# Attention's softmax reciprocals: a trip through DRAM in place of a ScalarE copy and transposes

## The chip, the cores and the metric

The kernel runs on one core of one Trainium2 chip. Time is device time in microseconds (us). A core has TensorE (PE, with its weight loads PEld), VectorE (DVE), ScalarE (ACT), GpSimd (POOL) and SyncE (SP). Here SP issues nearly all DMAs, in one queue that goes strictly in order: when an issue on SP has to wait, everything behind it waits too.

## What is computed

One layer over 2048 positions of width 1024, all in float32. The part that matters here is one of two groups of heads:

```
h   = RMSNorm(x);  z = h @ W_in
A   = gated MLP heads (8 heads)
B   = softmax(q k^T / 8 + c[t] - c[s]) v   for s <= t, 8 heads of width 64
x   = x + concat(A, B) @ W_out
x   = x + ConvFFN(RMSNorm(x));  out = RMSNorm(x)
```

Each row of the softmax has to be divided by its sum. The kernel multiplies the finished row of `p v` by the reciprocal of that sum.

## The kernel before

Every large product is made of three float32r matmuls (high and low parts). TensorE runs the projections, attention, the output projection, and the feed-forward layers one after the other. Attention is no phase of its own: a generator, `b_stream`, is advanced by one step after every 3.5 to 4.4 matmuls of the main work, so that attention's small matmuls lie between the main ones from about 120 us to 1470 us. `need` runs the generator on without waiting where the main work needs a finished block of 512 queries.

The pieces are (head `h`, query block `tb` of 512), eight heads in each of four blocks. A piece has two halves. `b_max` computes the scores with queries on partitions, and gets for each query the maximum and the sum of exponentials; its last instruction (L773, or L775 for `tb` = 0) writes the four reciprocals of each partition to the tile `rr`, which one pair of heads shares. `b_mix` computes the scores again with keys on partitions, and from them `p v` with the head's channels on partitions and queries along the free axis (tile `o` in PSUM). So the reciprocals lie on the wrong axis: query 128 a + p has its reciprocal on partition p, column a, and is wanted in column 128 a + p of all 64 partitions of its head. Pieces overlap: the order is `b_max` of a piece, then `b_mix` of the piece before it. `turn`, which `b_max` returns, is called at the fourth step of that `b_mix` and transposes the maxima (L779).

At the end of the second head of a pair, `b_mix` spreads the pair's reciprocals: ScalarE copies each of them 64 times into the tile `rw` (L835), the generator yields, four 128x128 transposes (L183, in `transpose4`) bring them into a PSUM bank, and VectorE multiplies the pair's `op` by that bank (L838). The result is split in two parts (tags `ph`, `pl`) and stored to `mixh` and `mixl`, from which the output projection loads it (`thi`, `tlo`). There are 16 pairs.

The bank comes from `scores`, which deals out three banks with the tag `s`, and later two more with the tag `dn`; attention's scores use the same ones. Keys come by `b_keys`: `m1` and `m2` (written `m<-kx` in the trace), and `v<-vd` for `b_mix`. There are two `m1` tiles, so the load of a key block has to wait on SP until TensorE is through with the block before the last. The order of instructions on each engine, SP's included, is fixed when the kernel is built, by a planner that works from a model of each instruction's and each transfer's time; a step's instructions go ahead of the main work's with a priority (`AHEAD_B`).

Of the kernel before, what the change touches and what calls it, by code (L numbers as in the profile page):

```python
# [8 lines left out]
F32 = mybir.dt.float32  # L9
F32R = mybir.dt.float32r  # L10
BF16 = mybir.dt.bfloat16
AF = mybir.ActivationFunctionType
ALU = mybir.AluOpType
# [5 lines left out]
P = 128  # L19
# [33 lines left out]
def f32(ap):  # L53
    return ap.bitcast(F32)
# [26 lines left out]
class Block:  # L81
# [134 lines left out]
    def constants(self):  # L216
        nc, a, tc = self.nc, self.a, self.tc
        cp = self.cpool = self.ctx.enter_context(tc.tile_pool(name="const", bufs=1))
        self.ident = cp.tile([P, P], F32, name="ident")
        make_identity(nc, self.ident)  # L220
        self.mhalf = cp.tile([P, 8], F32, name="mhalf")
        nc.gpsimd.memset(self.mhalf, -0.5)
        self.cols = cp.tile([P, 200], F32, name="cols")
        self.halo = cp.tile([P, 2 * NF, 2], F32, name="halo")
        nc.gpsimd.memset(self.halo, 0.0)
        dp = self.ctx.enter_context(tc.tile_pool(name="dram", bufs=1, space=DRAM))
        self.ones_d = dp.tile([2, HALF], F32, name="ones_d")
        t = lambda n, k, s: [dp.tile(s, F32, name=f"{n}{i}") for i in range(k)]
        self.qx = t("qx", 2, [8, 128, HALF])
        self.kx = t("kx", 2, [8, 132, HALF])  # L230
        self.cc = t("cc", 2, [8, 2, HALF])
        self.vd = t("vd", 2, [HALF, 8, P])
        self.mixh = t("mixh", 4, [D, TB])
        self.mixl = t("mixl", 4, [D, TB])
        self.rows_d = [t(f"rows{i}_", 8, [P, D]) for i in range(2)]
        self.act_d = [t(f"act{i}_", NF, [P, HALF]) for i in range(2)]
        self.tw_d = t("tw", NF // 2, [P, 2, D])

    def columns(self):

        nc, a = self.nc, self.a
        self.dma(self.cols, a["cols"])
        self.g_mix, self.g_ffn, self.sgb, self.cw0, self.cw1, self.cw2, self.cb = [
            self.cols[:, i:j] for i, j in ((0, 8), (8, 16), (16, 24), (24, 68), (68, 112), (112, 156), (156, 200))]
# [437 lines left out]
    def b_stream(self, pieces):  # L682

        todo = None
        for h, tb in pieces:
            while tb >= 2 and not self.ready:
                yield
            t1, t2, turn = yield from self.b_max(h, tb)
            if todo:
                yield from self.b_mix(*todo, turn)  # L690
                self.done += 1
            else:
                turn()
            todo = (h, tb, t1, t2, self.rr)
        yield from self.b_mix(*todo, None)
        self.done += 1

# [27 lines left out]
    def b_max(self, h, tb):  # L725

        nc, bp, pp = self.nc, self.bp, self.bpp
        hf, sl = tb // 2, slice((tb % 2) * TB, (tb % 2 + 1) * TB)
        self.T1.append(self.T1.pop(0))
        t1 = self.T1[0]  # L730
        t2 = self.til(self.mp, [P, TB], F32R, "t2")
        self.dma(f32(t1[0:64, :]), self.qx[hf][h, 0:64, sl])
        self.dma(f32(t1[64:66, :]), self.cc[hf][h, :, sl])
        self.dma(f32(t2), self.qx[hf][h, :, sl])
        nm = self.til(bp, [P, 4, 4], F32, "part")
        ls = self.til(bp, [P, 4, 4], F32, "ls")
        if h % 2 == 0:
            self.rr = self.til(bp, [P, 4, 2], F32, "rr")
        for sb in range(tb + 1):
            m1, m2 = self.b_keys(h, sb, False)  # L740
            for tt in range(4):
                ts = slice(tt * P, (tt + 1) * P)
                n = TB if sb < tb else (tt + 1) * P
                ps = self.scores([P, TB])
                nc.tensor.matmul(ps[:, :n], lhsT=t1[0:96, ts], rhs=m1[0:96, :n], start=True, stop=False)  # L745
                nc.tensor.matmul(ps[:, :n], lhsT=t2[:, ts], rhs=m2[:, :n], start=False, stop=True)  # L746
                dst = nm[:, tt, sb:sb + 1]
                if sb < tb:
                    nc.vector.tensor_reduce(dst, ps, axis=AX.X, op=ALU.min)  # L749
                else:  # L750
                    nc.vector.tensor_tensor_reduce(ps[:, :n], ps[:, :n], self.mask[:, 384 - tt * P:], 1.0, 3.0e38,
                                                   ALU.add, ALU.min, dst)

                nc.scalar.activation(ps[:, :n], ps[:, :n], AF.Exp, scale=-1.0, bias=dst, accum_out=ls[:, tt, sb:sb + 1])  # L754
                yield
        mx = self.til(bp, [P, 4], F32, "mx")
        if tb:
            nc.vector.tensor_reduce(mx, nm[:, :, 0:tb + 1], axis=AX.X, op=ALU.min)
        else:
            nc.vector.tensor_copy(mx, nm[:, :, 0])  # L760
        m8 = self.til(bp, [P, 4, 2], F32R, "m8")
        nc.vector.tensor_scalar(m8[:, :, 0], mx, -1.0, None, ALU.mult)
        nc.vector.scalar_tensor_tensor(m8[:, :, 1], mx, -1.0, f32(m8[:, :, 0]), op0=ALU.mult, op1=ALU.subtract)
        rr = self.rr[:, :, h % 2]
        if tb:
            k = slice(0, tb + 1)
            lw = self.til(bp, [P, 4, 4], F32, "lw")
            nc.vector.tensor_tensor(lw[:, :, k], mx.unsqueeze(2).broadcast_to([P, 4, tb + 1]), nm[:, :, k], op=ALU.subtract)
            nc.scalar.activation(lw[:, :, k], lw[:, :, k], AF.Exp)
            nc.vector.tensor_tensor(lw[:, :, k], lw[:, :, k], ls[:, :, k], op=ALU.mult)  # L770
            l1 = self.til(bp, [P, 4], F32, "l1")
            nc.vector.tensor_reduce(l1, lw[:, :, k], axis=AX.X, op=ALU.add)
            nc.vector.reciprocal(rr, l1)  # L773
        else:
            nc.vector.reciprocal(rr, ls[:, :, 0])  # L775

        def turn():
            pm = self.scores([8, P])
            nc.tensor.transpose(pm, f32(m8).rearrange("p a b -> p (a b)"), self.ident)  # L779
            nc.vector.tensor_tensor(t1[96:104, :].rearrange("p (a b) -> p a b", a=4),  # L780
                                    pm.unsqueeze(1).broadcast_to([8, 4, P]), self.rowsel, op=ALU.mult)

        return t1, t2, turn

    def b_mix(self, h, tb, t1, t2, rr, turn):

        nc, bp, pp = self.nc, self.bp, self.bpp
        po = self.til(pp, [P, TB], F32, "o")
# [3 lines left out]
        def pv():  # L792
            sc, c, v, ph, pl = late.pop(0)
            nc.tensor.matmul(po[:, c], lhsT=v, rhs=ph[:, c], start=sc == 0, stop=False)  # L794
            nc.tensor.matmul(po[:, c], lhsT=v, rhs=pl[:, c], start=False, stop=sc == ns - 1)  # L795

        for sc in range(ns):
            if sc == TURN and turn:
                turn()
            if sc % 4 == 0:  # L800
                m1, m2, v4 = self.b_keys(h, sc // 4, True)
            j = max(0, sc - 4 * tb)
            c = slice(j * P, TB)
            ks = slice((sc % 4) * P, (sc % 4 + 1) * P)
            ps = self.scores([P, TB])
            nc.tensor.matmul(ps[:, c], lhsT=m1[:, ks], rhs=t1[:, c], start=True, stop=False)  # L806
            nc.tensor.matmul(ps[:, c], lhsT=m2[:, ks], rhs=t2[:, c], start=False, stop=True)  # L807
            if sc >= 4 * tb:
                d = ps[:, j * P:(j + 1) * P]
                nc.vector.tensor_tensor(d, d, self.maskT, op=ALU.add)  # L810
            e = self.room([P, TB], F32, "e")
            nc.scalar.activation(e[:, c], ps[:, c], AF.Exp, scale=-1.0)  # L812
            if len(late) >= (LAG + 1 if self.more else LAG):
                pv()
            ph = self.room([P, TB], F32R, "ph")
            pl = self.room([P, TB], F32R, "pl")
            nc.scalar.activation(ph[:, c], e[:, c], AF.Copy)  # L817
            nc.vector.tensor_tensor(pl[:, c], e[:, c], f32(ph[:, c]), op=ALU.subtract)  # L818
            late.append((sc, c, v4[:, sc % 4, :], ph, pl))
            yield  # L820
# [6 lines left out]
        op = self.op  # L827
# [3 lines left out]
        if h % 2 == 0:  # L831
            return

        rw = self.til(self.mp, [P, 4, 2, 64], F32, "rw")
        nc.scalar.activation(rw, rr.unsqueeze(3).broadcast_to([P, 4, 2, 64]), AF.Copy)  # L835
        yield
        pr = self.transpose4(None, "s", [rw[:, i, :, :].rearrange("p a b -> p (a b)") for i in range(4)])
        nc.vector.tensor_tensor(op, pr, op, op=ALU.mult)  # L838
        oh = self.room([P, TB], F32R, "ph")
        ol = self.room([P, TB], F32R, "pl")  # L840
        self.split_sb(op, oh, ol)
# [669 lines left out]
```

## Time and profile before

| | |
|---|---|
| median of 3 runs | 2437.68 us (2436.88 to 2441.38) |
| profiled execution | span 2436.2 us, 1.5 us below that median; no other time of this execution is recorded |
| PE busy | 2409.5 us (99% of the span), 10984 matmuls |
| PEld, DVE, ACT, POOL busy | 81%, 72%, 55%, 13% |
| DMA | 400.51 MB, 164 GB/s mean |

The span runs from the first to the last instruction of the program. "Busy" of PE counts each matmul from its start to its modelled end, and neighbours overlap; how much of TensorE's time one matmul takes is read from the starts of those around it. In the lists of waits a row gives who waited, for whom, the total in us, how many times, and the longest. In the timeline a row gives start, duration, engine, line, operation and tiles; "x4" means four instructions merged in one row, and a bracket tells how long the engine was idle before and what ended that.

### The profile page before, as it was taken

To read this page: it belongs to the slowest core of one execution; us is meant where nothing else is said; L and a number is where in the kernel's file an instruction comes from. 1 tells how busy PE (TensorE), PEld (TensorE's weight loads), DVE (VectorE), ACT (ScalarE), POOL (GpSimd) and SP (SyncE) were. 2 spreads that over 40 slices of the span, in tenths; PEclk is the share of its full clock that TensorE was granted. 3 is DMA by queue.
4 is the path that set the end of the run, shared out by engine and by line. 5 is a ranking of instruction groups with operands and counts; after the bars stand their busy time and mean duration, and the time that the engine had idled before them with its cause. 6 is when DMAs were issued, how large, how long until landed. Compare 5 with 4: busy or idle time off the path is not lost.

```text
span 2436.2 us, 32591 instructions
## 1 busy us (share of the span) xinstructions
PE 2409.5 (99%) x10984; PEld 1982.9 (81%) x10984; DVE 1755.8 (72%) x3086; ACT 1348.5 (55%) x2635; POOL 312.5 (13%) x303
## 2 busy tenths in 40 slices
PE   9999999999999999999999999999999999999998
PEld 7788888788777888888888888888888888888887
DVE  5448776565557878878778774498888877957775
ACT  4347766544455556667676671365555555454443
POOL 3114140000213221111111201100000000000000
PEclk9999999999999999999999999999999999999999
DMA  8854646658756545554555436312222228538633
GB/s 290 276 140 123 199 120 174 169 170 280 215 158 213 187 154 164 163 166 144 179 175 180 157 123 236 140 56 80 85 87 87 78 92 311 164 99 297 206 115 121
DMA packets 245031, 400.51 MB, mean 164 GB/s; under 512 B 51240, under 2 KB 109736, under 8 KB 243440
## 3 DMA queue, kind: packets, MB, share of 16 engines
q1 hardware_dynamic: 239824, 374.31, 48.3%
q0 software_dynamic: 5040, 24.12, 2.5%
q8 instruction: 87, 1.43, 0.2%
q14 instruction: 80, 0.66, 0.1%
HBM read 304.76 MB, written 93.72 MB: 164 GB/s over the span
## 4 chain that ended last, share of the span: by engine, by line
PE 93%; DMA 3%; DVE 1%; ACT 1%; issue 0%; POOL 0%; SPq 0%; DVEq 0%; POOLq 0%; ACTq 0%
PE D L1351 16%; PE mm L210 14%; PE mm L208 14%; PE mm L212 14%; PE A L1149 3%; PE A L1150 3%; PE A L1151 3%; PE o L795 2%; PE o L794 2%; PE s L746 2%; PE s L745 2%; PE s L807 2%; PE s L806 2%; PE B L1150 2%; PE B L1151 2%; PE B L1149 2%
## 5 line engine op out<-in xcount | busy, mean ns | idle before, releaser
L210 PE MATMUL mm<-tlo,whi 128*128 128x512 f32 x912 | 358.1, 393 | 0.0
L208 PE MATMUL mm<-thi,whi 128*128 128x512 f32 x912 | 357.7, 392 | 0.0
L212 PE MATMUL mm<-thi,wlo 128*128 128x512 f32 x912 | 357.5, 392 | 0.0
L208 PE MATMUL mm<-whi,thi 128*128 128x512 f32 x640 | 252.9, 396 | 2.9 <-DMA thi<-mixh 2.2
L150 POOL TENSOR_SCALAR whi<-raw 128x1024 fp32r<-128x1024 f32 (+1 forms) x112 | 125.9, 1125 | 1005.1 <-PE mm L210 616.8
L210 PE MATMUL mm<-wlo,thi 128*128 128x512 f32 x640 | 251.3, 393 | 0.1
L212 PE MATMUL mm<-whi,tlo 128*128 128x512 f32 x640 | 251.0, 393 | 0.0
L754 ACT ACTIVATE s<-s,part 128x512 f32<-128x512 f32 (+3 forms) x261 | 154.6, 592 | 130.7 <-DVE part L749 81.4
L208 PEld LDWEIGHTS mm<-thi,whi 128*128 128x128 f32 x912 | 171.5, 188 | 35.7
L210 PEld LDWEIGHTS mm<-tlo,whi 128*128 128x128 f32 x912 | 171.5, 188 | 35.5
L212 PEld LDWEIGHTS mm<-thi,wlo 128*128 128x128 f32 x912 | 171.5, 188 | 34.8
L818 DVE TENSOR_TENSOR pl<-e,ph 128x512 fp32r<-128x512 f32 (+2 forms) x212 | 136.9, 655 | 76.8 <-ACT ph L817 39.3
L162 DVE TENSOR_TENSOR wlo<-raw,whi 128x1024 fp32r<-128x1024 f32 x104 | 136.2, 1309 | 54.0 <-POOL whi L150 53.6
L812 ACT ACTIVATE e<-s 128x512 f32<-128x512 f32 (+2 forms) x216 | 110.3, 527 | 95.3 <-DVE s L810 41.0
L208 PEld LDWEIGHTS mm<-whi,thi 128*128 128x128 f32 x640 | 120.6, 188 | 26.9 <-DMA thi<-mixh 2.5
L1351 PE MATMUL D<-wl,xh 128*128 128x512 f32 x368 | 141.3, 389 | 0.0
L1351 PE MATMUL D<-wh,xh 128*128 128x512 f32 x368 | 140.8, 389 | 0.2 <-DVE xo L1429 0.2
L212 PEld LDWEIGHTS mm<-whi,tlo 128*128 128x128 f32 x640 | 120.3, 188 | 24.3 <-DMA tlo<-mixl 0.7
L210 PEld LDWEIGHTS mm<-wlo,thi 128*128 128x128 f32 x640 | 120.6, 188 | 23.5 <-DVE wlo L162 0.5
L817 ACT ACTIVATE ph<-e 128x512 fp32r<-128x512 f32 (+2 forms) x212 | 116.3, 562 | 39.5 <-PE o L794 34.1
L1351 PE MATMUL D<-wh,xl 128*128 128x512 f32 x368 | 137.1, 389 | 0.0
L749 DVE TENSOR_REDUCE part<-s 128x1 f32<-128x512 f32 x149 | 98.2, 683 | 21.4 <-PE s L746 20.7
(1898 smaller groups left out, 5853.7 us busy)
## 6 DMA issues: line engine op xcount, KB each, us to landing
raw<-in_w_up_dram SPq DMA_DIRECT2D x72, 512.0 KB
m<-kx SPq DMA_DIRECT2D x133, 256.0 KB
m<-kx SPq DMA_DIRECT2D x160, 136.0 KB
x<-act SPq DMA_DIRECT2D x84, 256.0 KB
raw<-in_w_in_dram SPq DMA_DIRECT2D x36, 512.0 KB
v<-vd SPq DMA_DIRECT2D x66, 256.0 KB
raw<-in_w_out_dram SPq DMA_DIRECT2D x24, 512.0 KB
tw<-in_w_down_dram SPq DMA_DIRECT2D x11, 1024.0 KB
```

The lines of the kernel that those rows point to most:

```text
L150: self.cast_ins = self.nc.gpsimd.tensor_scalar(out, in_, 1.0, 0.0, ALU.mult, ALU.add).ins
L162: nc.vector.tensor_tensor(lo, raw, f32(hi), op=ALU.subtract)
L208: mm(ps, lhsT=ah[k], rhs=bh[k], start=k == 0, stop=False)
L210: mm(ps, lhsT=ah[k], rhs=bl[k], start=False, stop=False)
L212: self.last_mm = mm(ps, lhsT=al[k], rhs=bh[k], start=False, stop=k == n - 1).ins
L754: nc.scalar.activation(ps[:, :n], ps[:, :n], AF.Exp, scale=-1.0, bias=dst, accum_out=ls[:, tt, sb:sb + 1])
L817: nc.scalar.activation(ph[:, c], e[:, c], AF.Copy)
L818: nc.vector.tensor_tensor(pl[:, c], e[:, c], f32(ph[:, c]), op=ALU.subtract)
L1149: mm(ps, lhsT=xh[:, ks], rhs=yh[:, k, :], start=fresh and k == 0, stop=False, **kw)
L1150: mm(ps, lhsT=xh[:, ks], rhs=yl[:, k, :], start=False, stop=False, **kw)
L1151: mm(ps, lhsT=xl[:, ks], rhs=yh[:, k, :], start=False, stop=k == 3, **kw)
L1351: nc.tensor.matmul(bank[t], lhsT=x[i][:, ts], rhs=w[k], start=fresh and j == 0 and i + k == 0, stop=last and i == 1, **kw)
```

## The change

The reciprocals of a pair go to DRAM and come back spread:

- `rr` is laid out as [head of the pair, 4] on each partition; there are 16 new DRAM tiles `rl_d` of [2, 4, 128].
- `turn` of the pair's second head now begins with a store of `rr` to `rl_d`, in which each partition's eight numbers go to eight rows: 1024 pieces of 4 bytes. It is issued on SP.
- `b_mix` of the second head begins with two loads, each of one head's row of 512 numbers to 64 partitions (128 KB each), on SP, ahead of the head's keys. They wait for the store to land.
- At its end, the ScalarE copy, the yield and the four transposes are gone; VectorE multiplies `op` by the loaded tile in SBUF. That tile takes the place of `rw` (the same tag and size).

```
+        self.rl_d = t("rl", 16, [2, 4, P])
...
-            self.rr = self.til(bp, [P, 4, 2], F32, "rr")
+            self.rr = self.til(bp, [P, 2, 4], F32, "rr")
...
+        pair = self.rr
+
         def turn():
+            if h % 2:
+                self.dma(self.rl_d[4 * tb + h // 2].rearrange("b a p -> p (b a)"), pair.rearrange("p b a -> p (b a)"))
             pm = self.scores([8, P])
...
+        if h % 2:
+            rl = self.til(self.mp, [P, 4, P], F32, "rw")
+            for i in range(2):
+                self.dma(rl[64 * i:64 * i + 64, :, :], self.rl_d[4 * tb + h // 2][i:i + 1, :, :].broadcast_to([64, 4, P]))
         for sc in range(ns):
             if sc == TURN and turn:
                 turn()
...
-        rw = self.til(self.mp, [P, 4, 2, 64], F32, "rw")
-        nc.scalar.activation(rw, rr.unsqueeze(3).broadcast_to([P, 4, 2, 64]), AF.Copy)
-        yield
-        pr = self.transpose4(None, "s", [rw[:, i, :, :].rearrange("p a b -> p (a b)") for i in range(4)])
-        nc.vector.tensor_tensor(op, pr, op, op=ALU.mult)
+        nc.vector.tensor_tensor(op, rl.rearrange("p a b -> p (a b)"), op, op=ALU.mult)
```

More of the change, by code (lines that the diff above doesn't have):

```diff
@@ L693, in b_stream @@
                 turn()
-            todo = (h, tb, t1, t2, self.rr)
+            todo = (h, tb, t1, t2)
         yield from self.b_mix(*todo, None)
@@ L763, in b_max @@
         nc.vector.scalar_tensor_tensor(m8[:, :, 1], mx, -1.0, f32(m8[:, :, 0]), op0=ALU.mult, op1=ALU.subtract)
-        rr = self.rr[:, :, h % 2]
+        rr = self.rr[:, h % 2, :]
         if tb:
@@ L783, in b_max, with b_mix @@
         return t1, t2, turn
-    def b_mix(self, h, tb, t1, t2, rr, turn):
+    def b_mix(self, h, tb, t1, t2, turn):
         nc, bp, pp = self.nc, self.bp, self.bpp
```

## The prediction

> **What bounds the kernel now.** I read the page's busy shares first, then its chain of work that ended last, then the busy time by stage.
>
> ```profile
> span 2436.2 us, 32591 instructions
> ...
> PE 2409.5 (99%) x10984; PEld 1982.9 (81%) x10984; DVE 1755.8 (72%) x3086; ACT 1348.5 (55%) x2635; POOL 312.5 (13%) x303
> ...
> PE 93%; DMA 3%; DVE 1%; ACT 1%; issue 0%; POOL 0%; SPq 0%; DVEq 0%; POOLq 0%; ACTq 0%
> ```
>
> ```profile
> core 0: us, PE busy (x) PEld busy (x) DVE busy (x) ACT busy (x) POOL busy (x), PEclk, DMA share, GB/s
> 500.00:700.00 200.00, 191.94 (x873) 155.83 (x872) 116.36 (x236) 93.61 (x219) 21.26 (x24) 0.97 0.68 213
> 900.00:1100.00 200.00, 200.00 (x912) 165.61 (x911) 160.86 (x324) 131.72 (x299) 36.90 (x35) 1.00 0.53 169
> 1100.00:1300.00 200.00, 199.66 (x902) 164.19 (x901) 157.50 (x311) 140.86 (x312) 30.65 (x28) 1.00 0.51 164
> ```
>
> TensorE is the bound: 99% busy, 93% of the chain. From 900 to 1300 us, in the thick of attention, it has no idle time to speak of, while DVE and ACT are at 70 to 80%. Only one stage of attention has a hole, 500 to 700 us, with 8.1 us of idle PE and a granted clock of 0.97. So an instruction taken off TensorE is worth the slot that it took, and work taken off ACT is worth nothing by itself. The question is what a transpose's slot is, and whether the new DMAs leave TensorE waiting.
>
> **What goes: 64 transposes.** The instructions that touch the tile `rw` (each group with its count and its shortest, median and longest duration in ns):
>
> ```profile
> L183 PE MATMUL s<-ident,rw x60: 270/272/299, 188.1 to 1458.6; 128*128 128x128 f32 x60
> L835 ACT ACTIVATE rw<-rr x16: 615/632/638, 153.9 to 1417.1; 128x512 f32<-128x512 f32 x16
> L183 PE MATMUL dn<-ident,rw x4: 270/272/272, 1276.4 to 1276.7; 128*128 128x128 f32 x4
> ```
>
> One pair's four in PE's timeline:
>
> ```profile
> 1276.15 0.39 PE L212 MATMUL mm<-thi,wlo 128*128 128x512 f32 x1
> 1276.38 0.60 PE L183 MATMUL dn<-ident,rw 128*128 128x128 f32 x4
> 1276.74 0.48 PE L208 MATMUL mm<-thi,whi 128*128 128x512 f32 x1
> 1277.06 0.40 PE L795 MATMUL o<-pl+_2785_11790,v+_2777_11766 128*128 128x512 f32 x1
> ```
>
> An ordinary 512-column matmul starts 0.23 us after the one before it (1276.15 to 1276.38), though it is shown as lasting 0.39. From the first transpose to the second matmul behind them it is 1277.06 - 1276.38 = 0.68 us; one of those slots belongs to L208, so four transposes took 0.68 - 0.23 = 0.45 us. Sixteen pairs: 16 x 0.45 = 7.2 us. The durations, 64 x 0.272 = 17.4 us, are not what comes back. The Trainium skill, "TensorE: Matmul & The Clock Gate", section "Part 4: PE-mode transpose", puts one transpose at about 275 ns in a kernel; the duration agrees with that (272), but 64 x 0.275 would give 17.6 us, and the starts say 0.11 us for one.
>
> ACT loses 16 x 0.632 = 10.1 us. It is 66 to 70% busy in the two later stages quoted, so I count 0. The multiplication L838 keeps its size; its operand moves from PSUM to SBUF. Its duration and who waited for it:
>
> ```profile
> L838 DVE TENSOR_TENSOR op<-s,op x15: 681/692/693, 192.6 to 1471.2; 128x512 f32<-128x512 f32 x15
> ...
>   PE s L745: 0.7, 1
> ```
>
> I count 0 for the multiplication itself. PE's one wait of 0.7 us was for the bank that the transposes had filled; that bank is now never taken, so 0.7 us goes, and I see nothing late behind it but scores that go on. The yield that goes shortens the generator by 16 steps; the pacing of a saturated PE changes nothing in the sum: 0.
>
> **What comes: 16 stores, 32 loads, all on SP.** Nearest issue costs are the `vd` transfers (the store, also in 1024 pieces, of 256 bytes), nearest landings are in the chain, in order of time (start, us, what):
>
> ```profile
> L100 SPq DMA_DIRECT2D v<-vd x66: 359/371/2442, 137.1 to 1450.5; - x66
> L100 SPq DMA_DIRECT2D vd<-vn x32: 513/524/3190, 114.8 to 462.9; - x32
> ```
>
> ```profile
> 673.88 3.30 DMA mixh<-ph
> 677.20 4.28 DMA thi<-mixh
> 722.61 6.40 DMA rows<-acc
> 751.90 8.32 DMA m<-kx
> ```
>
> SP's own time: 16 x (0.52 + 2 x 0.37) = 20 us in some 1300, hidden, as SP is mostly waiting (below). The transfers: 32 x 128 KB = 4.2 MB, at the mean 164 GB/s 26 us over the same 1300 us where DMA is about half busy: 0. The store's 4-byte pieces are not in the trace. From above, the mean packet of the hardware queue:
>
> ```profile
> q1 hardware_dynamic: 239824, 374.31, 48.3%
> ```
>
> 0.483 x 16 x 2436.2 us / 239824 = 78 ns for 1.56 KB on average; 1024 / 16 x 78 ns = 5.0 us of each DMA engine per store; from below nothing. A 4-byte piece is nearer to nothing, so I take about 1 us, lying beside other transfers. The Trainium skill, "DMA: Bandwidth & Descriptors", section "Rules for kernel authors", speaks against this store: a last axis that is not contiguous becomes one descriptor for each element. That is already so counted, in 1024 pieces; no run here shows such a store yet.
>
> The real risk is order. Two waits enter SP's queue: the store waits for the reciprocal on DVE, and the loads wait for the store to land. Around one pair:
>
> ```profile
> 921.61 0.18 DVE L773 RECIPROCAL rr<-l 128x4 f32<-128x4 f32 x1
> ```
>
> ```profile
> 921.82 0.63 ACT L835 ACTIVATE rw<-rr 128x512 f32<-128x512 f32 x1 [0.23 <-DVE rr L773]
> ```
>
> ```profile
> 922.97 0.33 SPq L100 DMA_DIRECT2D raw<-in_w_up_dram  x1
> 924.06 0.69 SPq L100 DMA_DIRECT2D m<-kx  x2
> ```
>
> ```profile
> 930.00 0.39 PE L806 MATMUL s<-t,m 128*128 128x512 f32 x1
> ```
>
> The planner put the copy L835 right behind the reciprocal, long before the transposes, so I expect the store there and the loads as soon as it believes the store landed. The store fits between 921.8 and the next issue at 922.97. The loads are wanted only by L838, after the last step of that head's whole `b_mix`: covered, so that what they cost is what stands behind them. Behind a load that waits stand the weights (`raw`) and the keys, and the keys have 930.00 - 924.06 = 5.9 us until TensorE wants them, of which a load of that kind takes some 4.3 (the `thi` row): 1.6 us of cover. What SP and PE waited for so far:
>
> ```profile
> SPq L100 <- PE s L746: 164.5, 64, 7.4
> SPq L100 <- DMA rows<-acc: 45.9, 11, 7.5
> SPq L100 <- DMA vd<-vn: 3.9, 1, 3.9
> ```
>
> ```profile
> PE mm L208 <- DMA thi<-mixh: 2.2, 1, 2.2
> PE s L745 <- DMA t<-qx: 1.2, 3, 0.6
> PE s L746 <- DMA t<-qx: 1.1, 1, 1.1
> PE s L806 <- DMA m<-kx: 0.5, 1, 0.5
> ```
>
> SP has stood still 45.9 us for the landing of stores to DRAM, and PE's waits for attention's loads (1.2 + 1.1 + 0.5 = 2.8 us) are all that can have come of it. If each new store holds SP for 3.9 us, that is 62 us, and in the same proportion 62 / 45.9 x 2.8 = 3.8 us of PE; if the planner is generous, 0. I take the middle, 1.9 us; the other end is the slower rival.
>
> **Sum.** -7.2 - 0.7 + 1.9 = -6.0 us on the span: 2430.2. The median of the runs lies 1.5 above this span, so 2431.7 us, 0.25% less.
>
> **Rivals.**
>
> *More than the slots.* The transposes' bank was held from 1276.4 until L838. In the hole before 681.5 attention's scores ran with one bank fewer, and PE came back at half pace (0.42 us between starts):
>
> ```profile
> 678.89 0.42 PE L746 MATMUL s<-m,t 128*128 128x256 f32 x1
> 681.53 0.79 PE L208 MATMUL mm<-whi,thi 128*128 128x512 f32 x1 [2.22 <-DMA thi<-mixh]
> 682.12 0.63 PE L210 MATMUL mm<-wlo,thi 128*128 128x512 f32 x1
> 682.54 0.63 PE L208 MATMUL mm<-whi,thi 128*128 128x512 f32 x1
> ```
>
> The hole is 8.1 us idle and 0.03 x 200 = 6 us of clock. If half of it closes, 7 us more: 2424.7. Against: what ends it is the store and reload of `mixh` (3.30 + 4.28 us), which stay.
>
> *All of the durations* come back (the page's reading): 2437.7 - 17.4 = 2420.3. The starts speak against it.
>
> *Eaten.* On the eight pairs with `tb` = 2 and 3, where key loads run close to their use, TensorE loses 0.75 us each: 6 - 7.9 = -1.9, 2435.8.
>
> *Nothing.* Attention's own chain, not the slot count, sets the pace, and the slots turn to idle: 2437.7. PE at 200.00 of 200 us speaks against it.
>
> *Slower: SP stands behind the store.* If the planner believes in an earlier landing than the real one, the load goes ahead of the keys. With the 3.9 us row, keys arrive 3.9 - 1.6 = 2.3 us late. On eight pairs that is 18 us: +10.5, 2448; on all sixteen 37 us: +29, 2467. It decides from (7.9 + 4.9) / 16 = 0.8 us per pair. For it: SP's 45.9 us for `rows`. Against: PE waited for keys once, 0.5 us, though SP waited 164.5 us for their buffers.
>
> **How the numbers follow.** 0.2% (4.9 us) is about what a measurement of this kernel can tell from no change. The forecast, with its cost between 0 and 3.8 us, runs from 2429.8 to 2433.6: chance 0.47, of which 0.38 beyond 0.2% and 0.09 within. More than the slots 0.14, all durations 0.02, eaten 0.17, nothing 0.07, slower 0.13. Faster 0.38 + 0.14 + 0.02 = 0.54; same 0.09 + 0.17 + 0.07 = 0.33; slower 0.13. The range 2423 to 2441 leaves out the slower case, the full durations and a tail of the larger gain, some 0.17.
>
> **What would show it.** Right: no L183 on `rw`; PE's sum of busy time down by about 17 us while the span falls by about 6; PE's wait for L838 gone; SP waits for `rl` short, and PE's wait for `m<-kx` still below 2 us. Wrong: SP waiting 2 us or more at each pair for `rl<-rr`, `m<-kx` issued later against its use, and PE waits for keys; or a store whose pieces hold the DMA engines so long that other landings stretch; or a hole around 670 us that grew or closed.

## The result, and the profile after

The changed kernel took 2567.51 us (median of 4 runs, 2565.21 to 2571.17), against 2439.09 us for the kernel before (4 runs, 2436.88 to 2441.38): a ratio of 1.0528, 95% interval 1.0516 to 1.0541. It is slower by 128 us, where 6 us less were forecast. Ratios, here and below, leave out single executions that took far longer than the others of their kernel (2663 us and more). The page of the changed kernel: span, busy shares, the chain's shares by engine, and the hardware queue.

```profile
span 2567.5 us, 32570 instructions
...
PE 2440.6 (95%) x10920; PEld 2002.6 (78%) x10920; DVE 1756.9 (68%) x3086; ACT 1341.8 (52%) x2619; POOL 316.3 (12%) x303
...
q1 hardware_dynamic: 259024, 378.57, 48.0%
...
PE 81%; DMA 11%; DVE 4%; ACT 2%; issue 1%; SPq 1%; POOL 1%; DVEq 0%; POOLq 0%; ACTq 0%
```

The 64 transposes are gone (10920 matmuls for 10984), and yet PE's busy sum rose by 31 us: a matmul that runs at half pace is shown as longer (0.63 us below, where 0.39 is usual). DMA went from 3% to 11% of the chain, though the queue's share of the engines did not rise (48.3% before, 48.0% now). More idle TensorE, hardly more DMA work: something is held up. By stage:

```profile
900.00:1100.00 200.00, 184.91 (x829) 152.33 (x827) 145.85 (x293) 117.48 (x258) 35.76 (x33) 0.96 0.50 155
1100.00:1300.00 200.00, 191.78 (x848) 157.12 (x849) 153.34 (x301) 127.33 (x293) 35.46 (x31) 0.98 0.53 164
```

The stage that had no idle time (200.00 of 200) now has 15.1 us of it and a granted clock of 0.96. What PE and SP waited for (total, times, longest):

```profile
PE s L815 <- DMA m<-kx: 49.9, 7, 9.9
PE s L746 <- DMA t<-qx: 28.6, 7, 8.7
PE s L746 <- DMA t<-cc: 9.9, 3, 5.6
PE dn L815 <- DMA m<-kx: 4.9, 1, 4.9
```

```profile
SPq L100 <- DMA rl<-rr: 159.3, 16, 12.7
```

PE's waits for attention's loads (keys, queries, and the small `t<-cc`), 2.8 us before, are about 100 us. SP stood 16 times behind the store's landing (`rl<-rr`), 10 us each time on average. Two landings of the store as the chain of work shows them (start, us): the longest there, and the one of the next views:

```profile
259.35 14.04 DMA rl<-rr
...
993.76 11.49 DMA rl<-rr
```

One pair: SP's timeline, then PE's.

```profile
993.76 0.37 SPq L100 DMA_DIRECT2D rl<-rr  x1
1005.32 1.09 SPq L100 DMA_DIRECT2D rw<-rl  x2
1006.50 0.54 SPq L100 DMA_DIRECT2D raw<-in_w_up_dram  x1
1007.13 1.99 SPq L100 DMA_DIRECT2D m<-kx  x4
```

```profile
1003.99 0.39 PE L210 MATMUL mm<-tlo,whi 128*128 128x512 f32 x1
1013.56 0.76 PE L815 MATMUL s<-t,m 128*128 128x512 f32 x1 [9.18 <-DMA m<-kx]
...
1014.55 0.63 PE L799 MATMUL o<-ph,v 128*128 128x512 f32 x1
1014.97 0.63 PE L212 MATMUL mm<-thi,wlo 128*128 128x512 f32 x1
1015.40 0.63 PE L208 MATMUL mm<-thi,whi 128*128 128x512 f32 x1
```

The store is issued at 993.76; the loads of `rl` behind it wait until 1005.32; the weights and four key loads stand behind those loads; TensorE runs dry at 1004.4 and waits 9.18 us for a key. It then comes back at half pace: 0.42 us between starts, where 0.23 is usual. The Trainium skill, "TensorE: Matmul & The Clock Gate", section "Part 1: The HAM clock gate (the "warmup" mystery)", says that an idle window of about 3.4 us halves TensorE's rate; these starts agree with it. Over the span, by my own count of the trace, distances of more than 0.9 us between PE's starts sum to 127.7 us (17.5 before) and starts at half pace cost about 24 us (1.5 before): 110 + 23, less the 7 us of the transposes' slots, is 126 of the 131 us between the two spans.

What the DMA engines did in that time, two microseconds a row; the last column is GB/s, the one before it the DMA share:

```profile
991.00:993.00 2.00, 2.00 (x11) 1.65 (x10) 1.25 (x7) 1.66 (x4) 0.00 (x0) 1.00 0.61 218
993.00:995.00 2.00, 2.00 (x10) 1.68 (x9) 1.96 (x5) 1.51 (x3) 1.35 (x1) 1.00 0.12 3
995.00:997.00 2.00, 2.00 (x11) 1.54 (x10) 1.97 (x5) 1.36 (x3) 0.00 (x0) 1.00 0.12 1
997.00:999.00 2.00, 2.00 (x10) 1.66 (x9) 1.97 (x4) 0.88 (x2) 0.00 (x0) 1.00 0.00 0
999.00:1001.00 2.00, 2.00 (x10) 1.68 (x9) 0.79 (x3) 0.98 (x2) 0.57 (x1) 1.00 0.04 4
1001.00:1003.00 2.00, 2.00 (x10) 1.65 (x10) 0.63 (x2) 1.76 (x4) 0.00 (x0) 1.00 1.69 193
```

From the store on next to nothing moves for 8 us (0 to 4 GB/s), and the engines are shown as nearly idle (a share of 0.00 to 0.12). Here SP issued nothing behind the store, so this view alone cannot tell an empty queue from a blocked one. That is the question of the experiments.

### The profile page after: what moved, and what is told of

It reads as the page before. It is cut to its first block, busy times and chain, and to the rows that moved or that the text cites. A ratio compares the mean times of both kernels' runs of the same rounds, so it can differ in the third digit from the quotient of the medians.

```text
span 2567.5 us, 32570 instructions
## 1 busy us (share of the span) xinstructions
PE 2440.6 (95%) x10920; PEld 2002.6 (78%) x10920; DVE 1756.9 (68%) x3086; ACT 1341.8 (52%) x2619; POOL 316.3 (12%) x303
## 4 chain that ended last, share of the span: by engine, by line
PE 81%; DMA 11%; DVE 4%; ACT 2%; issue 1%; SPq 1%; POOL 1%; DVEq 0%; POOLq 0%; ACTq 0%
PE D L1356 15%; PE mm L212 11%; PE mm L208 11%; PE mm L210 11%; DMA m<-kx 3%; DMA rl<-rr 3%; PE A L1154 3%; PE A L1156 3%; PE A L1155 3%; PE o L800 2%; PE o L799 2%; PE s L747 2%; PE s L746 2%; PE s L815 2%; PE s L816 2%; PE B L1156 2%
## 5 line engine op out<-in xcount | busy, mean ns | idle before, releaser
L210 PEld LDWEIGHTS mm<-tlo,whi 128*128 128x128 f32 x912 | 173.0, 190 | 35.8
L815 PE MATMUL s<-t,m 128*128 128x512 f32 (+2 forms) x249 | 94.2, 383 | 50.0 <-DMA m<-kx 49.9
```

Source lines behind the costliest of these rows:

```text
L210: mm(ps, lhsT=ah[k], rhs=bl[k], start=False, stop=False)
```

## Experiments

Two theories stood at first. *SP's wait*: the loads of `rl` hold SP's queue, and the keys behind them come late. *The store itself*: it holds up every other transfer. Ratios below are against the kernel before, run on the same chip, with 95% intervals. "Landing" is the time from the store's issue to the last of its semaphore updates in the trace, worked out by me over the 16 stores.

**First four: take the parts apart.** *e1_late* has the change, with its loads placed behind the last key load of their own `b_mix`:

```
+            if h % 2 and sc == ns - 4:
...
+                with self.tc.issue_after(self.key_ins):
+                    ...  # the two loads of rl
```

> The two loads of a pair are ordered on SP behind the last key load of their own head's b_mix, instead of ahead of its first; the store stays. In the program's order this moves the loads 13 to 42 DMAs behind the store for the twelve pairs with tb >= 1; for the four pairs with tb = 0 (one key block only) they still stand right behind it or with two DMAs between. Theory 1 (SP stands still for the landing of the store, and keys and queries queue behind it): the twelve pairs lose nothing more, the four keep their idle PE, which in the changed kernel is 28.8 us of gaps over 0.9 us and some 6 us of half pace; less 7 us of slots that makes about +28 us, ratio 1.011, SP's wait for rl<-rr about 46 us instead of 159. Theory 2 (the 4-byte pieces or the DRAM writes stretch the other transfers, whatever SP does): ratio 1.03 or more, PE's waits for m<-kx stay near 50 us.

*e2_ones* stores, but its two loads read a constant, so that they do not wait for the store (attention's rows are then multiplied by one, not by their reciprocals):

```
-                self.dma(rl[64 * i:64 * i + 64, :, :], self.rl_d[4 * tb + h // 2][i:i + 1, :, :].broadcast_to([64, 4, P]))
+                self.dma(rl[64 * i:64 * i + 64, :, :].rearrange("p a b -> p (a b)"), self.ones_d[i:i + 1, 0:TB].broadcast_to([64, TB]))
```

> The store stays, and the two loads stay where they are and of the same size, but read the rows of ones that the kernel wrote to DRAM at its start, so that they wait for no store (attention's rows are then not divided by their sums). All the new traffic, none of the new wait. Theory 1 (the wait on SP): about 7 us less than before, ratio 0.997, SP waits for rl<-rr gone. Theory 2 (the traffic of the store or of the loads disturbs other transfers): still slower by 2% or more.

*e3_32b* stores each partition's eight numbers in one piece of 32 bytes (128 pieces); its loads wait as in the change. They read 512 numbers in a row, so that rows get other queries' reciprocals: it measures a cost and is no version to use.

```
-        self.rl_d = t("rl", 16, [2, 4, P])
+        self.rl_d = t("rl", 16, [P, 8])
...
+                self.dma(self.rl_d[4 * tb + h // 2], pair.rearrange("p b a -> p (b a)"))
...
+                self.dma(rl[64 * i:64 * i + 64, :, :].rearrange("p a b -> p (a b)"), self.rl_d[4 * tb + h // 2].rearrange("(b p) e -> b (p e)", b=2)[i:i + 1, :].broadcast_to([64, TB]))
```

> The store goes to a DRAM tile laid out as [128, 8], so that each partition's eight reciprocals are one piece of 32 bytes: 128 pieces instead of 1024, the same 4 KB. The loads read 512 consecutive numbers of it and still wait for it (the reciprocals then come in another order, so rows are scaled by other queries' numbers). It tells what makes the landing long. Theory 1a (1024 pieces of 4 bytes): landing falls from 9 to 15 us to 2 to 4 us, about what the cover of a key load takes, and the ratio to 0.998 to 1.010. Theory 1b (any store to DRAM lands so late in this traffic): SP's wait for rl<-rr stays near 159 us and the ratio near 1.05.

*e4_store* is the kernel before, copy and transposes and all, with the 16 stores added and nothing that reads them:

```
+            if h % 2:
+                self.dma(self.rl_d[4 * tb + h // 2].rearrange("a b p -> p (a b)"), pair.rearrange("p a b -> p (a b)"))
```

> The kernel before, with the copy on ScalarE and the transposes, plus only the sixteen stores in 1024 pieces of 4 bytes at the same place; nobody reads them. Theory 1: ratio 1.000 (within 0.2%), PE's waits as before. Theory 2: the pieces alone cost 2 to 5%.

| | ratio | median us | SP's wait for `rl` | landing, median |
|---|---|---|---|---|
| the change | 1.0528 (1.0516 to 1.0541) | 2567.5 | 159.3 us | 11.2 us |
| e1_late | 1.0351 (1.0333 to 1.0368) | 2525.4 | 35.8 us | 11.3 us |
| e2_ones | 1.0350 (1.0334 to 1.0365) | 2521.5 | 9.5 us | 11.4 us |
| e3_32b | 0.9971 (0.9960 to 0.9982) | 2430.7 | 26.4 us | 1.8 us |
| e4_store | 1.0367 (1.0351 to 1.0382) | 2527.2 | 0.3 us | 11.5 us |

The store alone, with no reader and no transpose removed, costs 3.7%, 88 us. Taking most of SP's wait away (e2) leaves 3.5%; moving the loads back (e1) does the same, so the first theory's figure for e1 was missed by far. With 32-byte pieces the whole loss is gone, though SP still waits 16 times, more briefly:

```profile
SPq L100 <- DMA rl<-rr: 26.4, 16, 3.9
```

In e4_store no reader stands in SP's queue. Its queue, and the transfers of the same stretch:

```profile
963.10 0.37 SPq L100 DMA_DIRECT2D rl<-rr  x1
964.26 0.33 SPq L100 DMA_DIRECT2D raw<-in_w_up_dram  x1
965.34 6.69 SPq L100 DMA_DIRECT2D m<-kx  x4
```

```profile
961.00:963.00 2.00, 2.00 (x11) 1.65 (x10) 1.96 (x6) 1.37 (x4) 1.22 (x1) 1.00 0.28 96
963.00:965.00 2.00, 2.00 (x11) 1.58 (x10) 1.97 (x4) 1.30 (x3) 0.00 (x0) 1.00 0.23 2
965.00:967.00 2.00, 2.00 (x11) 1.63 (x10) 1.94 (x3) 1.94 (x4) 0.00 (x0) 1.00 0.00 0
967.00:969.00 2.00, 2.00 (x10) 1.67 (x9) 1.40 (x4) 0.01 (x1) 0.57 (x1) 1.00 0.44 37
969.00:971.00 2.00, 2.00 (x10) 1.67 (x9) 0.88 (x2) 2.00 (x4) 0.00 (x0) 1.00 0.35 29
971.00:973.00 2.00, 0.44 (x2) 0.02 (x1) 0.79 (x2) 2.00 (x5) 0.00 (x0) 1.00 1.13 47
973.00:975.00 2.00, 0.00 (x0) 0.00 (x0) 0.00 (x0) 0.78 (x2) 0.00 (x0) 0.86 0.41 35
975.00:977.00 2.00, 0.00 (x0) 0.00 (x0) 0.00 (x0) 0.00 (x0) 0.00 (x0) 0.50 0.82 297
```

Half a megabyte of weights is issued at 964.26 and keys from 965.34, and still little moves until 975 (0 to 47 GB/s): the queue is not empty, it is blocked, and PE falls from 2.00 to 0.00 on the way. The packets in the kept trace show where. The store's own are soon through: they all start between 0.9 and 1.6 us after its issue and are shown with some 7 ns each. The packets of weights and keys behind them then take up to 3.4 us each, where the median of a 4 KB packet in the kernel before is 0.24 us (from 120 to 1400 us). PE's waits say what it lacked:

```profile
PE s L811 <- DMA m<-kx: 37.7, 7, 7.4
```

**Next four: what of the store.** Number of pieces, their size, their spacing, or writing as such? *f1_16b* keeps 16 bytes together (256 pieces) and lets VectorE read the loaded tile with a stride, which puts the queries back in their order:

```
-        self.rl_d = t("rl", 16, [2, 4, P])
+        self.rl_d = t("rl", 16, [2, P, 4])
...
+                self.dma(self.rl_d[4 * tb + h // 2].rearrange("b p a -> p b a"), pair)
...
+        o4 = op.rearrange("p (a b) -> p a b", a=4)
+        nc.vector.tensor_tensor(o4, rl.rearrange("p b a -> p a b"), o4, op=ALU.mult)
```

> The changed kernel with the DRAM tile laid out as [2, 128, 4], so that a partition's four reciprocals of one head are one piece: 256 pieces of 16 bytes instead of 1024 of 4. The loads bring each head's 512 numbers in the order (p, a), and the multiplication on VectorE reads them with a stride of four to put them right, so the whole is the same computation. Theory A (the DMA engines stand still in proportion to the number of pieces): a standstill of some 2.5 us instead of 10, inside the cover of the keys; ratio 0.996 to 0.999. Theory B (any piece under some size between 16 and 32 bytes costs the full standstill): slower by 2% or more.

The other three are e4_store with the store replaced. *f2_pad* puts the 1024 pieces 64 bytes apart:

```
+        self.rl_d = t("rl", 16, [8, P, 16])
...
+                self.dma(self.rl_d[4 * tb + h // 2].rearrange("e p w -> p e w")[:, :, 0:1], pair.rearrange("p a b -> p (a b)").unsqueeze(2))
```

> The kernel before plus only the store, as in e4_store, in 1024 pieces of 4 bytes, but each piece goes to a place of its own 64 bytes from its neighbours (64 KB of DRAM for one store instead of 4 KB). Theory C (neighbouring pieces collide in the same few lines of DRAM and go one after another): the standstill goes, ratio 1.000 to 1.005. Theory A' (each piece costs its writer the same wherever it goes): as e4_store, 1.03 to 1.04.

*f3_half* stores 512 pieces, packed as in the change:

```
+                self.dma(self.rl_d[4 * tb + h // 2].rearrange("a p -> p a"), pair.rearrange("p a b -> p (a b)")[:, 0:4])
```

> As e4_store, but only one head's half of the reciprocals: 512 pieces of 4 bytes. Theory A (proportional to the pieces): standstill of some 5 us instead of 10; what is left over the cover of the key loads (about 5 us, as e4_store lost some 5 us of each 10) is near nothing, ratio 1.000 to 1.012. If the standstill is one price for any such store, ratio 1.03 or more.

*f4_read* has, in the program's place of the store, a load of 1024 pieces of 4 bytes:

```
+                self.dma(self.til(bp, [P, 8], F32, "rx"), self.ones_d[0:1, :].rearrange("a (e p) -> p (a e)", p=P))
```

> The kernel before plus, in place of each store, one load of 1024 pieces of 4 bytes from DRAM into a small tile in SBUF that nobody reads: the same count of pieces, the other way. Theory W (it is the writes of 4 bytes to DRAM): ratio 1.000 to 1.005. Theory P (it is the pieces as such): 1.02 to 1.04.

| | ratio | landing, median |
|---|---|---|
| f1_16b: whole change, 256 x 16 bytes | 0.9998 (0.9989 to 1.0007) | 3.6 us |
| f2_pad: store alone, 1024 x 4, 64 bytes apart | 1.0011 (1.0001 to 1.0020) | 4.6 us |
| f3_half: store alone, 512 x 4, packed | 1.0332 (1.0317 to 1.0346) | 10.8 us |
| f4_read: load alone, 1024 x 4, packed | 1.0043 (1.0027 to 1.0058) | 3.9 us |

It is not the number of pieces: half of them cost nearly as much (f3), and all of them cost almost nothing once they lie apart (f2). Nor is it another order of the work: by the tiles in their traces, f2_pad, f3_half and e4_store issue the same other transfers on SP and the same matmuls, in the same order. In f2_pad the store's packets start and last as in e4_store, but in the stretch of the table further down no packet behind them takes more than 1.5 us.

f4_read does not test what it was meant to. Its loads wait for nothing, and the planner put all sixteen between 69 and 121 us, before the place of the first store (154 us). Eleven of them stand on SP ahead of the first load of `x` below, which the kernel before issues at 86.29. ScalarE waits for that `x`, and PE has its one long hole behind it. So most of the 0.4% (10.9 us) comes from the loads' place on SP:

```profile
90.02 6.56 SPq L100 DMA_DIRECT2D rx<-ones_d  x5
...
99.55 1.28 SPq L100 DMA_DIRECT2D x<-in_x_dram  x1
```

```profile
104.44 1.06 ACT L344 ACTIVATE ln<-x 128x1024 bf16<-128x1024 f32 x1 [11.13 <-DMA x<-in_x_dram]
```

```profile
PE mm L208 <- DVE st L396: 10.3, 1, 10.3
```

What these reads do to other traffic can still be seen. From 112 to 120 us two of them are issued (113.18 and 117.77) among other transfers, and the 2-us rows show 282 to 351 GB/s. This one begins just behind the second:

```profile
118.00:120.00 2.00, 2.00 (x9) 1.63 (x8) 0.00 (x0) 0.00 (x0) 0.00 (x0) 0.82 1.08 338
```

So such a read does not block what stands behind it, as the packed store does. What sixteen of them would cost amid attention was not measured.

f1_16b ends level with the kernel before, just outside the 0.996 to 0.999 of its first theory, although e3_32b gained 0.29%. Its SP waits are longer (42.6 us for 26.4), and PE waits more for queries (9.0 us for 5.9, about half of the difference; the rest was not settled):

```profile
SPq L100 <- DMA rl<-rr: 42.6, 15, 5.0
```

```profile
PE s L746 <- DMA t<-qx: 4.7, 2, 3.7
PE s L747 <- DMA t<-qx: 4.3, 2, 2.6
```

**Third four: spacing, and a better version.** *g1_late16* joins f1_16b's pieces with e1_late's later loads.

> f1_16b with the loads ordered on SP behind the last key load of their head's b_mix, as in e1_late: pieces of 16 bytes and, for the twelve pairs with tb >= 1, no wait on SP; the same computation as before. If what ate f1_16b's gain is SP's wait for the landing (42.6 us there, with some 9 us of PE's waits for t<-qx), ratio 0.996 to 0.998, SP's wait for rl<-rr under 15 us (the four pairs with tb = 0 keep it). If the saved slots are worth nothing: 1.000.

*g2_own* is f2_pad with each partition's eight pieces in a stretch of 64 bytes of its own, 8 bytes apart; *g3_s16* has the pieces 16 bytes apart, four to 64 bytes:

```
+        self.rl_d = t("rl", 16, [P, 8, 2])     # g2_own
+        self.rl_d = t("rl", 16, [8, P, 4])     # g3_s16
```

> The kernel before plus only the store, in 1024 pieces of 4 bytes, laid out as [128, 8] with a distance of 8 bytes between neighbours: a stretch of 64 bytes takes the eight pieces of one partition, not sixteen of sixteen partitions. If only the number of pieces that share a stretch of 64 bytes counts (16 in e4_store and f3_half, 4 in f1_16b, 1 in f2_pad), the standstill is about half that of e4_store, 5 us, landing 6 to 8 us, ratio 1.002 to 1.015. If it takes writers of different partitions meeting in one stretch, nothing is lost: ratio 1.000 to 1.003, landing 3 to 5 us.

> The kernel before plus only the store, in 1024 pieces of 4 bytes, 16 bytes apart: four pieces, of four partitions, in each stretch of 64 bytes. By the count of pieces in one stretch: standstill about 2.5 us, landing 3.5 to 5.5 us, ratio 1.000 to 1.004, near f2_pad. If 4-byte neighbours cost as much at 16 bytes as at 4: ratio 1.03.

*g4_hybrid* is g1_late16 with the ScalarE copy and the transposes kept for the four pairs of the first query block, where 12.0 of the 42.6 us of SP's waits in f1_16b lay, and 5.3 of PE's 9.0 us for queries.

> As g1_late16, but the four pairs with tb = 0, whose loads cannot be put far behind their store, keep the copy on ScalarE and the four transposes. Twelve pairs save 12 x 0.45 = 5.4 us and no load waits on SP: ratio 0.997 to 0.998. If the four early pairs' waits cost less than their four times 0.45 us of slots, g1_late16 is the faster of the two; I expect this one to be faster by 0 to 4 us.

Results: g1_late16 0.9987 (0.9978 to 0.9995), 2434.37 us, PE waiting 7.9 us for queries and SP 11.2 us for `rl`; g2_own 1.0131 (1.0115 to 1.0147), landing 7.7 us; g3_s16 1.0009 (0.9999 to 1.0018), landing 5.1 us; g4_hybrid 1.0026 (1.0017 to 1.0036), 2444.49 us. So g1_late16 is faster than the changed kernel, and than the kernel before by 0.13%, with an interval just clear of 1. That is short of the 0.996 to 0.998 expected: SP's wait went as forecast, PE's waits for queries hardly fell. g4_hybrid missed its expectation: it took away most of the early waits (queries 1.8 us), but its whole order was planned anew, and PE waits for keys elsewhere:

```profile
PE s L816 <- DMA m<-kx: 4.5, 3, 3.2
PE s L817 <- DMA m<-kx: 1.8, 1, 1.8
```

The two rows sum to 6.3 us, where its median is 10.1 us above g1_late16's; the rest was not settled.

**Last: close together, or crowded in the whole?** g2_own still has its pieces 8 bytes apart over 8 KB. *h1_iso* leaves the eight pieces of a partition in 64 bytes and puts the partitions 1024 bytes apart, store alone:

```
+        self.rl_d = t("rl", 16, [P, 128, 2])
...
+                self.dma(self.rl_d[4 * tb + h // 2][:, 0:8, 0:1], pair.rearrange("p a b -> p (a b)").unsqueeze(2))
```

> The kernel before plus only the store: as in g2_own each partition's eight pieces of 4 bytes lie within 64 bytes, 8 bytes apart, but the partitions' stretches are now 1024 bytes apart, so that any stretch of 512 or 1024 bytes holds eight pieces (as many or fewer than in f2_pad) while a stretch of 64 bytes still holds eight. If it is stretches of about 64 bytes that pieces have to share, landing about 7.7 us (minimum about 6) and ratio 1.008 to 1.016, as g2_own. If it is the density over a wider stretch (512 bytes or more), landing about 4.6 us (minimum about 2.6) and ratio 1.000 to 1.002, as f2_pad.

h1_iso came to 1.0292 (1.0270 to 1.0315), landing 11.1 us, outside both ranges expected. Wide distances between the stretches do not help, so crowding over 512 bytes or more is not what costs; how pieces share a much shorter stretch is. Why it is worse than g2_own, with as many in each stretch, stays open. The same store of all variants, in GB/s of the 2-us rows from its issue on:

| | pieces in 64 bytes | GB/s | ratio |
|---|---|---|---|
| e3_32b | 2 | 2, 120, 247, 235, 199 | 0.9971 |
| f1_16b | 4 | 6, 22, 196, 309, 283 | 0.9998 |
| f2_pad | 1 | 2, 82, 329, 263, 129 | 1.0011 |
| g3_s16 | 4 | 2, 55, 343, 280, 152 | 1.0009 |
| g2_own | 8 | 2, 18, 41, 142, 359 | 1.0131 |
| h1_iso | 8 | 18, 41, 96, 72, 200 | 1.0292 |
| f3_half | 16 | 17, 0, 37, 25, 16 | 1.0332 |
| e4_store | 16 | 2, 0, 37, 29, 47 | 1.0367 |

In e3_32b and f1_16b readers wait for the store; the six kernels below have the store alone. By the tiles in their traces, these six issue everything else on SP, and the matmuls on PE, in the same order, so that f2_pad, g3_s16, g2_own, h1_iso and e4_store differ only in where the same 1024 pieces go. How long the shared stretch is, they do not tell. Going by the count alone it is shorter than 128 bytes, where g3_s16 and h1_iso both have eight pieces and yet differ. But the count in 64 bytes goes with the distance between neighbours (4, 8, 16 or 64 bytes), and "more than one piece in 16 bytes" sorts the table into loss and no loss as well as "eight or more in 64".

Three of its rows, four microseconds behind the store, of f2_pad, g3_s16 and g2_own:

```profile
928.00:930.00 2.00, 2.00 (x11) 1.65 (x10) 1.57 (x4) 0.11 (x1) 0.57 (x1) 1.00 0.85 329
```

```profile
932.00:934.00 2.00, 2.00 (x10) 1.66 (x9) 1.40 (x4) 0.03 (x1) 0.57 (x1) 1.00 0.95 343
```

```profile
943.00:945.00 2.00, 2.00 (x11) 1.65 (x10) 1.29 (x4) 0.29 (x1) 0.57 (x1) 1.00 0.71 41
```

## Why the prediction was wrong

- **The bound and the slots: right, as far as the runs can tell.** e3_32b, with all of the change but the size of the pieces and the order of the numbers, is 7 us faster by its ratio (4.4 to 9.8 by the interval), where 7.2 us for the slots and 0.7 us for the bank were forecast; between e4_store and e2_ones, which differ by slots and loads, it is 5.7 us. So a transpose was worth about its slot and not its 272 ns. That ACT's 10 us were worth nothing fits this, but was not measured alone. The multiplication stayed at 692 ns (L843):

```profile
L843 DVE TENSOR_TENSOR op<-rw,op x16: 679/692/1154, 201.3 to 1588.8; 128x512 f32<-128x512 f32 x16
```

- **The store's pieces: the step that failed.** "A 4-byte piece is nearer to nothing, so I take about 1 us, lying beside other transfers" put the term at 0. It is +88 us (e4_store). The first half was right: the store's packets are shown with 7 ns each and have all started 1.6 us after the issue. The overlap was wrong: next to nothing moves beside the store or behind it until 8 to 12 us are over. I asked only how long the store keeps the engines busy, with 5.0 us as the upper bound, and not what becomes of the transfers behind it. The number of pieces, on which the working rested, is not what counts (f2_pad, f3_half).
- **SP's wait: right in kind, too small.** The loads were put right behind the store, as forecast, and the sum had 1.9 us for it. Its landing was taken from the row `vd<-vn`, 3.9 us; it was 9 to 15 us, so SP waited 159.3 us and not 62. That is worth 2567.5 - 2521.5 = 46 us, the change against e2_ones (42 us against e1_late). The slower rival had the direction, and its mechanism explains a third; at 2467 us its end was 100 us short, as it priced the store by that same row.
- **The sum** with the measured terms: -7 + 88 + 46 = +127, against 128 measured. This checks less than it seems: 46 is the change less e2_ones, so that only the slots are measured twice (7 us by e3_32b, 5.7 us by e4_store less e2_ones).
- **The other rivals.** e3_32b's gain speaks against "nothing", and its size against "all of the durations". "Eaten" comes near what f1_16b shows, by waits for queries and not for keys. Of the larger gain by a closing hole little came: from 650 to 700 us PE is busy for 45.14 us in e3_32b and 42.94 before. The bank that it named was free from 672.9 us (the end of L838), before the wait of 2.22 us that ends the hole.
- **The signs named** for a wrong forecast were the ones seen: SP waiting 2 us or more at each pair, PE waiting for keys, "a store whose pieces hold the DMA engines so long that other landings stretch". The last had been named, and given no chance of its own.

The Trainium skill's rule on a strided last axis ("DMA: Bandwidth & Descriptors", "Rules for kernel authors") points the right way, but its count of descriptors does not give the loss: 1024 of them cost 0.1% spaced out and 3.7% packed. The Trainium skill, "DMA: Bandwidth & Descriptors", section "Specifications", has transfers under 512 bytes do a read-modify-write. All pieces here are under that, 16 and 32 bytes too, and no loss is seen with those (0.9998 and 0.9971). No run here shows what the memory does with a small piece; only that sharing a stretch is what costs.

## What to carry to other kernels

Price a scattered store not by its bytes or its pieces but by whether many of them share a stretch of 64 bytes or less of DRAM (eight in 64 bytes cost here, four did not): if they do, ask what every other transfer of the next 10 us is worth. Keep 16 bytes or more together, which was enough here, and let the reader put the order right, as VectorE does in f1_16b with a strided read (1071 ns instead of 692, on an engine that is 72% busy in the kernel before). On a queue that goes in order, a load that waits for a store belongs behind the loads that wait for nothing. And look in the trace where the planner put a new transfer before reading its cost: f4_read's loads were nowhere near the place meant.

## What the runs showed of the hardware

- One store of 1024 pieces of 4 bytes, packed into 4 KB of DRAM, held back nearly all DMA traffic of the core for 8 to 12 us (e4_store: 0 to 47 GB/s, with weights and keys queued), though its own packets had all started after 1.6 us. The same pieces 64 bytes apart let it go on after 2 us at 82 GB/s and then at 329 (f2_pad).
- 512 of them did nearly the same harm as 1024 (1.0332 for 1.0367), and eight to a stretch with the stretches 1 KB apart more than eight to a stretch without gaps (1.0292 for 1.0131).
- Reading 1024 pieces of 4 bytes did not stop other traffic: 282 to 351 GB/s around two such loads (f4_read, 112 to 120 us).
